# Two feed-forward layers: another order for the first token tile, the token forms and the first products of the down projection

## The chip, the cores and the metric

The kernel runs on one core of one Trainium2 chip. The time is that of the device in microseconds (us), the median of several executions, lower being better. All sums and differences are held in 32-bit floats.

## The reference, cut to what matters

The whole reference is a hybrid block (feed-forward, sparse and forgetting attention, memory attention, feed-forward) and then an attention and a pooling layer, on 512 tokens of width 1024. The change concerns the two feed-forward layers (FFN1 at the start of the kernel, FFN2 in its middle), the loads ahead of FFN1, and a small table of attention biases that is made beside FFN1:

```
def rmsnorm(x, g):
    y = x32 * lax.rsqrt(jnp.mean(x32 * x32, axis=-1, keepdims=True) + RMS_EPS)
    return (y * g).astype(x.dtype)
def swiglu(h, w_gate, w_up, w_down):
    return (jax.nn.silu(h @ w_gate) * (h @ w_up)) @ w_down
x = x + 0.5 * swiglu(rmsnorm(x, ffn1_norm[l]), ffn1_w_gate[l], ffn1_w_up[l], ffn1_w_down[l])
```

D_MODEL is 1024, D_FF is 2816, so a feed-forward layer has 8 slices of 128 input features (KD) and 22 tiles of 128 hidden features (NF).

## The kernel before

Tokens lie along the free dimension, features along the 128 partitions. Every 32-bit product is made of three: each operand is split into a high and a low part of TensorE's reduced 32-bit type (`split`, L83: a copy on ScalarE (ACT) makes the high part at L78, a subtraction on VectorE (DVE) the low part at L81 or L89), and `three` (L116) issues high x high, high x low and low x high. The token tiles are `xh[k]`, `xl[k]`. A weight tile of 128 x 1024 is loaded on SyncE's queue (SP, L112), split, and used for 24 matmuls of 512 columns (`gemm_steps`, L121). There are three buffers each of raw, high and low weights (`wr`, `wh`, `wl`).

Ahead of FFN1 (L1513 on) the eight token tiles are loaded and split, the gate weights of tile 0 after token tile 0, its up weights after the last token tile. The squares of the tokens (for the norm) are made on ACT, and summed on GpSimd (POOL, L223).

`ffn` (L428) then has these stages:

- **The plain part**: hidden tiles f = 0 to 3, one gate product and one up product each, 24 matmuls of 512 columns apiece. The scale of the norm (`rstd`, L257) is taken after four slices of tile 1. `up_gate` (L438) multiplies by it, applies silu and stores the result `hx[f]`.
- **The forms** (class `Halves`, L355): sums and differences of quarters of the token matrix, called t1, t2, t3 and t4, four slices each. For each k two token tiles are loaded again from DRAM on SP's queue (L365, three buffers `g`), scaled in place on ACT, combined in four operations on DVE (L371 to L374) and split. t1 overwrites the right halves of `xh[0..3]`, `xl[0..3]`, which the plain part still reads until its end. The class is called after the plain part.
- **The seven-product part** (`seven`, L387): the other 18 hidden tiles in nine pairs, for the gate and then the up weights of a pair: seven products of 12 matmuls of 256 columns instead of eight. The order of products is raw left, t3, t2, t1, raw, t4, raw. One of its weight tiles gets its low part by a DMA on POOL's queue that accumulates (L399).
- **The down part**: first all `hx` are split (`halves`, L481: 22 splits, f = 0 on), then eight output tiles follow. The first two run side by side, eight slices of one, eight of the other, and so on. At outputs 3 and 4 FFN1 also runs `bias_rows` (L604): small loads, two small products, and a copy of the result to 128 rows in DRAM (`rep`, L619), all its DMAs on SP's queue.

TensorE (PE) runs in the order of the program; the other engines and the queues are ordered by a planner from the program's order, buffers and its own costs.

## Time and profile before

| | us |
|---|---|
| median of 3 runs | 1708.16 (1707.75 to 1710.77) |
| the profiled execution, its own time | 1711.25 |
| its span, first to last instruction | 1709.5 |
| PE busy | 1652.4 (97% of the span) |
| VectorE (DVE) busy | 1150.6 (67%) |
| ScalarE (ACT) busy | 908.5 (53%) |
| mean granted TensorE clock | 0.986 of 2.4 GHz |

PE busy time counts a matmul until its modelled end, at whatever clock it ran; so time is lost in two ways: PE idle (some 57 us in all), and PE busy at the lower clock. In the rows below times are microseconds from the span's start; a timeline row gives start, duration, engine, line, operation, output and inputs, how many, and in brackets how long the engine had been idle and what it waited for. PEld is the weight load of a matmul.

### The profile page before, as it was taken

Reading aid. Unit: us, or ns where it says so; the run is one execution under the profiler, and the core shown is the slowest. Engines: PE = TensorE matmul, PEld = TensorE weight load, DVE = VectorE, ACT = ScalarE, POOL = GpSimd, SP = SyncE. Lnnn points to the kernel's source line nnn. Section 1 sums busy time; section 2 is a strip of 40 time slices with the busy share of each in tenths; the row PEclk is TensorE's granted clock in tenths of the full one; section 3 lists DMA queues with packets and bytes.
Section 4 is the critical chain, followed back from the end, with each engine's and each line's share of the span. In section 5 each row is a group of like instructions: output and inputs, shape, how many; then the busy total and the mean of one; then the engine's idle time right before and its main releaser. Section 6 shows DMA issues by size and latency. Waiting matters only on the chain.

```text
span 1709.5 us, 25566 instructions
## 1 busy us (share of the span) xinstructions
PE 1652.4 (97%) x9596; PEld 1434.8 (84%) x9596; DVE 1150.6 (67%) x2114; ACT 908.5 (53%) x1580; POOL 308.4 (18%) x395
## 2 busy tenths in 40 slices
PE   8899999989999999999999998999999999999997
PEld 6699998778777888887988877999888888878887
DVE  7688875336786677776655457788743698866674
ACT  6566663225675566645534455666533477744343
POOL 2011100003322232203001201112011044420001
PEclk9899999999999999999999998999999999999999
DMA  7578853533343122136531545888344311143232
GB/s 233 146 180 189 188 129 107 184 101 98 109 127 125 56 75 80 32 114 207 175 133 44 204 131 145 184 182 180 93 132 128 125 62 62 63 147 116 93 118 77
DMA packets 78987, 216.92 MB, mean 127 GB/s; under 512 B 9398, under 2 KB 15368, under 8 KB 78864
## 3 DMA queue, kind: packets, MB, share of 16 engines
q1 hardware_dynamic: 61648, 175.44, 32.3%
q0 software_dynamic: 10368, 28.32, 10.0%
q10 hardware_dynamic: 6848, 11.54, 1.8%
q8 instruction: 75, 1.23, 0.3%
q14 instruction: 48, 0.39, 0.1%
HBM read 202.64 MB, written 15.24 MB: 127 GB/s over the span
## 4 chain that ended last, share of the span: by engine, by line
PE 84%; DVE 7%; ACT 3%; issue 2%; DMA 2%; POOL 1%; SPq 0%; DVEq 0%; ACTq 0%; POOLq 0%
PE mm L117 15%; PE mm L118 15%; PE mm L119 15%; PE mm L352 6%; PE sc L352 6%; PE tr L352 5%; PE pv L352 4%; DVE wl L81 1%; PE tr L119 1%; PE tr L565 1%; PE tr L117 1%; PE tr L118 1%; PE pv L321 1%; PE pv L322 1%; PE pv L323 1%
## 5 line engine op out<-in xcount | busy, mean ns | idle before, releaser
L78 ACT ACTIVATE wh<-wr 128x1024 fp32r<-128x1024 f32 (+2 forms) x256 | 256.1, 1002 | 361.5 <-PE mm L118 193.6
L81 DVE TENSOR_TENSOR wl<-wr,wh 128x1024 fp32r<-128x1024 f32 (+2 forms) x219 | 254.3, 1163 | 138.8 <-ACT wh L78 136.9
L117 PE MATMUL mm<-xh,wh 128*128 128x512 f32 x584 | 244.9, 419 | 7.1 <-ACT wh L78 5.7
L118 PE MATMUL mm<-xl,wh 128*128 128x512 f32 x584 | 233.7, 400 | 0.2
L119 PE MATMUL mm<-xh,wl 128*128 128x512 f32 x584 | 233.0, 399 | 0.0
L223 POOL TENSOR_TENSOR acc<-acc,t 128x512 f32<-128x512 f32 (+1 forms) x55 | 75.0, 1371 | 519.5 <-ACT t L222 519.3
L118 PE MATMUL mm<-h,wh 128*128 128x512 f32 x352 | 140.4, 399 | 3.6 <-DVE h L81 3.6
L117 PE MATMUL mm<-h,wh 128*128 128x512 f32 x352 | 140.2, 398 | 3.8 <-ACT wh L78 3.8
L119 PE MATMUL mm<-h,wl 128*128 128x512 f32 x352 | 140.5, 399 | 0.8 <-DVE wl L81 0.8
L117 PEld LDWEIGHTS mm<-xh,wh 128*128 128x128 f32 x584 | 112.2, 192 | 25.7 <-ACT wh L78 5.7
L119 PEld LDWEIGHTS mm<-xh,wl 128*128 128x128 f32 x584 | 111.0, 190 | 26.5 <-DVE wl L81 0.2
L118 PEld LDWEIGHTS mm<-xl,wh 128*128 128x128 f32 x584 | 111.6, 191 | 19.3 <-DVE xl L89 2.4
L78 ACT ACTIVATE ph<-tr 128x512 fp32r<-128x512 f32 (+3 forms) x136 | 63.1, 467 | 51.8 <-PE tr L565 45.3
L81 DVE TENSOR_TENSOR pl<-tr,ph 128x512 fp32r<-128x512 f32 (+3 forms) x136 | 72.0, 530 | 24.0 <-ACT ph L78 23.0
L117 PEld LDWEIGHTS mm<-h,wh 128*128 128x128 f32 x352 | 67.3, 191 | 20.1 <-ACT wh L78 4.8
L118 PEld LDWEIGHTS mm<-h,wh 128*128 128x128 f32 x352 | 67.2, 191 | 19.7 <-DVE h L81 4.3
L555 POOL TENSOR_SCALAR P<-P,sm 128x128 f32<-128x128 f32 (+1 forms) x96 | 53.6, 571 | 155.3 <-DVE sm L552 70.1
L119 PEld LDWEIGHTS mm<-h,wl 128*128 128x128 f32 x352 | 67.4, 191 | 16.5 <-DVE wl L81 1.2
L81 DVE TENSOR_TENSOR pl<-wr,ph 128x1024 fp32r<-128x1024 f32 x36 | 44.1, 1225 | 38.5 <-ACT ph L78 38.3
L546 ACT ACTIVATE P<-S,nmx 128x128 f32<-128x128 f32 (+1 forms) x96 | 53.5, 557 | 23.7 <-DVE nmx L542 21.9
L117 PE MATMUL mm<-yh,wh 128*128 128x512 f32 (+1 forms) x176 | 64.5, 366 | 0.5 <-DVE xs L1467 0.4
L118 PE MATMUL mm<-yl,wh 128*128 128x512 f32 (+1 forms) x176 | 64.4, 366 | 0.4 <-DVE yl L89 0.2
(446 smaller groups left out, 4691.6 us busy)
## 6 DMA issues: line engine op xcount, KB each, us to landing
wr<-in_mfm_dram SPq DMA_DIRECT2D x32, 512.0 KB, 3.5
wr<-in_f2gu_dram SPq DMA_DIRECT2D x26, 512.0 KB, 3.5
wr<-in_f1gu_dram SPq DMA_DIRECT2D x24, 512.0 KB, 4.2
xd<-xs ACTq DMA_DIRECT2D x40, 256.0 KB, 2.0
r<-in_f1gu_dram SPq DMA_DIRECT2D x18, 512.0 KB, 4.3
wl<-in_f1gu_dram POOLq DMA_DIRECT2D x18, 512.0 KB, 6.9
r<-in_f2gu_dram SPq DMA_DIRECT2D x18, 512.0 KB, 4.3
wl<-in_f2gu_dram POOLq DMA_DIRECT2D x18, 512.0 KB, 7.2
```

The lines of the kernel that those rows point to most:

```text
L78: nc.scalar.activation(o, i, AF.Copy, scale=scale)
L81: (eng or nc.vector).tensor_sub(o, i, h.bitcast(F32))
L117: nc.tensor.matmul(o, sh, mh, start=start, stop=False)
L118: nc.tensor.matmul(o, sh, ml, start=False, stop=False)
L119: nc.tensor.matmul(o, sl, mh, start=False, stop=stop)
L223: (nc.vector if last else nc.gpsimd).tensor_add(acc, acc, q[:, :n])
L321: mm(b, sh[k][:, tk], hi[:, c], start=first, stop=False, skip_group_check=True)
L322: mm(b, sh[k][:, tk], lo[:, c], start=False, stop=False, skip_group_check=True)
L323: mm(b, sl[k][:, tk], hi[:, c], start=False, stop=last, skip_group_check=True)
L352: nc.tensor.matmul(o, w[:, c], x, start=start and k + z == 0, stop=stop and k == 3 and z == 2, skip_group_check=True)
L546: nc.scalar.activation(w, sc[:, :n], AF.Exp, scale=-1.0, bias=nmx[:, i : i + 1], accum_out=sm[:, i : i + 1])
L555: nc.gpsimd.tensor_scalar(w, w, sm[:, z : z + 1], 1.0, op0=OP.mult, op1=OP.mult)
```

## The change

- **First tile**: nine matmuls on zeros stand first. The token tiles and both weight tiles of f = 0 are loaded and split in a fixed order: token 0; the first quarters of gate and up weights; token 1; the second quarters; tokens 2 and 3; the halves left; tokens 4 to 7. Gate and up products go slice by slice in turns. The gains are loaded on ACT's queue. The squares come after the copy of tile 1's last weights and are summed on DVE; the loads of `ident` and the causal mask come after them. The norm's scale is taken in tile 2 of FFN1 (tile 1 of FFN2, as before).
- **Forms**: `Halves` is called after tile 1 of the plain part instead of after tile 3, in both layers. Its loads use the buffers `xs`. t1 is kept as a 32-bit tile, and split into `xh`, `xl` (`finish`) after the plain part.
- **Plain tiles' results** are split at once (`first`), so `halves` has 18 tiles left, f = 4 on.
- **Down part**: the two first outputs alternate after 4, 4, 8 and 6 slices instead of 8, 8 and 6.
- `bias_rows` runs at tiles 2 and 3 of the plain part instead of at outputs 3 and 4 of the down part.

```diff
+WARM = 9
...
-            split(hi[:, c], lo[:, c], raw[:, c])
+            last_high[0] = copy(hi[:, c], raw[:, c])
+            low(lo[:, c], raw[:, c], hi[:, c])
...
+            self.first = [up.tile([P, 256], F32, name=nm("t1")) for _ in range(4)]
             for k in range(4):
                 ab = []
                 for m in (k, k + 4):
-                    x = up.tile([P, S], F32, tag="g", bufs=3, name=nm("g"))
+                    x = tp.tile([P, S], F32, tag="xs", bufs=3, name=nm("xs"))
                     nc.sync.dma_start(x, cur[0][P * m : P * (m + 1), :])
                     copy(x, x, gcol(gain, m))
                     ab.append(x)
                 a, b = ab
                 one, two = slice(0, 256), slice(256, 512)
-                u, v = tmp(), tmp()
-                nc.vector.tensor_sub(u[:, one], a[:, one], a[:, two])
-                nc.vector.tensor_add(u[:, two], b[:, two], u[:, one])
+                u, v = self.first[k], tmp()
+                t = tmp()
+                nc.vector.tensor_sub(u, a[:, one], a[:, two])
                 nc.vector.tensor_sub(v[:, one], a[:, two], b[:, two])
-                nc.vector.tensor_sub(v[:, two], b[:, one], u[:, two])
-                split(xh[k][:, two], xl[k][:, two], u[:, one])
-                split(*self.t["t2"][k], u[:, two])
+                nc.vector.tensor_add(t[:, one], b[:, two], u)
+                nc.vector.tensor_sub(v[:, two], b[:, one], t[:, one])
                 split(*self.t["t3"][k], v[:, one])
+                split(*self.t["t2"][k], t[:, one])
                 split(*self.t["t4"][k], v[:, two])
+
+        def finish(self):
+            for k in range(4):
+                split(xh[k][:, 256:], xl[k][:, 256:], self.first[k])
...
+        half = (lead + NF) // 2
+        hold = 2 if ws else 1
+        extra = aside() if aside else iter(())
...
+            first = [[lp.tile([P, S], F32R, name=nm("h")) for _ in range(2)]
+                     for _ in range(1, lead)]
+            r = new_rstd()
+            first.insert(0, [tp.tile([P, S], F32R, tag="rstd", bufs=3, name=nm("h"))
+                             for _ in range(2)])
...
-                nc.vector.tensor_mul(hx[f], a, pu)
...
-                x = Halves(up, gain)
...
+                h = tmp()
+                nc.vector.tensor_mul(h, a, pu)
+                split(*first[f], h)
+                hh.append(first[f][0])
+                hl.append(first[f][1])
+
+            forms = ExitStack()
+            held = []
+            for f in range(lead):
+                if f in (2, 3):
+                    next(extra, None)
+                pg, pu = (pvb(), pvb()) if f == hold == 2 else (mmb(), trb())
+                if ws and f == 0:
+                    both = [gemm_steps(b, None, KD, xh, xl, ws=w) for b, w in zip((pg, pu), ws)]
+                    for _ in range(KD):
+                        for steps in both:
+                            advance(steps, 1)
+                    for steps in both:
+                        drain(steps)
+                    held.append((f, pg, pu))
+                    continue
+                steps = gemm_steps(pg, wgu[f, 0], KD, xh, xl)
+                if f == hold:
+                    advance(steps, 4)
+                    rstd(acc, r)
+                    for h in held:
+                        up_gate(*h)
+                drain(steps)
+                gemm(pu, wgu[f, 1], KD, xh, xl)
+                if f < hold:
+                    held.append((f, pg, pu))
+                else:
+                    up_gate(f, pg, pu)
+                if f == 1:
+                    if ws:
+                        acc = acc(last_high[0])
+                    rp = forms.enter_context(area("raw", "right"))
+                    up = forms.enter_context(area("up", "right"))
+                    x = Halves(up, gain)
+            x.finish()
...
+                g1, g2 = (tp.tile([P, S], F32, tag="xs", bufs=3, name=nm("g")) for _ in range(2))
...
-                halves(p1, range(half))
+                halves(p1, range(lead, half))
...
-                        for n in (KD, KD, NF - 2 * KD):
+                        for n in (4, 4, KD, NF - 2 * KD):
...
-                        if m in (3, 4):
-                            next(extra, None)
...
-        hot = [tmp()[:33, :320] for _ in range(2)]
+        hot = [new_acc()[:33, :320] for _ in range(2)]
...
-    nc.sync.dma_start(gains[:, : len(GAINS) * KD], A["gains"])
+    nc.scalar.dma_start(gains[:, : len(GAINS) * KD], A["gains"])
...
+    begun = ExitStack()
+    xp0 = begun.enter_context(area("x0", "right"))
+    with area("w0") as wp0:
+        warm = wp0.tile([P, S], BF16, name="warm")
+        nc.vector.memset(warm, 0.0)
+        wb = pvb()
+        for _ in range(WARM):
+            nc.tensor.matmul(wb, warm[:, :P], warm, start=True, stop=True)
         x0 = [xp0.tile([P, S], F32, name=f"x0{k}") for k in range(KD)]
 
+        raw = [wp0.tile([P, DM], F32, name=f"w0{i}") for i in range(2)]
+        ws = [(wp.tile([P, DM], F32R, tag="wh", name=nm("wh")),
+               wp.tile([P, DM], F32R, tag="wl", name=nm("wl"))) for _ in range(2)]
+
+        keep = tc.keep_in_program_order
+
+        def begin(hi, lo, raw, src, gain=1.0):
+            keep(nc.sync.dma_start(raw, src))
+            last = keep(copy(hi, raw, gain))
+            keep(nc.vector.scalar_tensor_tensor(lo, raw, gain, hi.bitcast(F32), op0=OP.mult,
+                                                op1=OP.subtract))
+            return last
+
         def token_tile(k):
-            nc.sync.dma_start(x0[k], A["xT"][P * k : P * (k + 1), :])
-            split(xh[k], xl[k], x0[k], gcol("ffn1", k))
-
+            return begin(xh[k], xl[k], x0[k], A["xT"][P * k : P * (k + 1), :], gcol("ffn1", k))
+
+        cuts = [slice(0, 256), slice(256, 512), slice(512, 1024)]
         token_tile(0)
-        ws.append(weights(A["f1gu"][0, 0], cuts=2))
-        for k in range(1, KD):
-            token_tile(k)
-        ws.append(weights(A["f1gu"][0, 1], cuts=2))
-        acc0 = new_acc()
-        for k in range(KD):
-            square_in(acc0, x0[k], k == 0)
+        for z, c in enumerate(cuts):
+            for i in range(2):
+                begin(ws[i][0][:, c], ws[i][1][:, c], raw[i][:, c], A["f1gu"][0, i][:, c])
+            for k in ((1,), (2, 3), (4, 5, 6, 7))[z]:
+                token_tile(k)
...
-    nc.sync.dma_start(ident, A["c_ident"])
-    nc.vector.tensor_copy(ident_bf, ident)
     rep = dr.tile([8, P, 640], F32, name="rep")
-    cm = tmp()
-    nc.sync.dma_start(cm[:, :P], A["c_causal"])
-    nc.vector.tensor_copy(cmask_bf, cm[:, :P])
-
-    acc = ffn(A["f1gu"], A["f1d"], acc0,
+
+    def first_acc(behind):
+        acc = new_acc()
+        with tc.issue_after(behind.ins):
+            for k in range(KD):
+                square_in(acc, x0[k], k == 0, True)
+        parts = pieces(acc)
+        begun.close()
+        nc.sync.dma_start(ident, A["c_ident"])
+        nc.vector.tensor_copy(ident_bf, ident)
+        cm = tmp()
+        nc.sync.dma_start(cm[:, :P], A["c_causal"])
+        nc.vector.tensor_copy(cmask_bf, cm[:, :P])
+        return parts
+
+    acc = ffn(A["f1gu"], A["f1d"], first_acc,
               lambda m, t, a: prep_tile(m, t, gcol("mix", m), a), "ffn1", ws=ws, aside=bias_rows)
     with ExitStack() as late:
         tokens = mem_tokens(late)
```

## Rows read from the trace of the kernel before

**Rows 1.** The page, part 1: busy time, share of the span, instructions.
```profile
PE 1652.4 (97%) x9596; PEld 1434.8 (84%) x9596; DVE 1150.6 (67%) x2114; ACT 908.5 (53%) x1580; POOL 308.4 (18%) x395
```
**Rows 2.** Waits of PE over the span: in total, times, longest.
```profile
PE mm L352 <- ACT t L78: 15.0, 4, 4.2
...
PE mm L118 <- DVE h L81: 3.6, 2, 1.8
```
**Rows 3.** Timeline of the first 25 us: PE, DVE and POOL.
```profile
4.67 0.75 DVE L89 SCALAR_TENSOR_TENSOR xl<-x,gains,xh 128x512 fp32r<-128x512 f32 x1 [1.93 <-ACT xh L78]
...
5.73 0.79 PE L117 MATMUL mm<-xh,wh 128*128 128x512 f32 x1 [5.73 <-ACT wh L78]
...
9.89 7.80 DVE L89 SCALAR_TENSOR_TENSOR xl<-x,gains,xh 128x512 fp32r<-128x512 f32 x6 [0.38 <-ACT xh L78]
...
13.61 0.63 PE L119 MATMUL mm<-xh,wl 128*128 128x512 f32 x1
...
14.04 0.63 PE L117 MATMUL mm<-xh,wh 128*128 128x512 f32 x1
...
15.67 6.56 POOL L223 TENSOR_TENSOR acc<-acc,t 128x512 f32<-128x512 f32 x4 [0.89 <-ACT t L222]
...
17.39 0.40 PE L119 MATMUL mm<-xh,wl 128*128 128x512 f32 x1
```
**Rows 4.** Timeline of PE: where tile 1 of FFN1 begins.
```profile
24.70 0.40 PE L117 MATMUL mm<-xh,wh 128*128 128x512 f32 x1
```
**Rows 5.** Transfer rate of the first 60 us, in 40 slices of 1.5 us.
```profile
GB/s 0 112 335 270 290 399 407 397 394 246 19 0 0 0 44 327 307 403 324 284 232 344 385 251 262 276 223 64 109 288 280 202 0 0 76 186 251 266 234 74
```
**Rows 6.** Timeline of PE around the first seven products of FFN1.
```profile
58.90 0.28 PE L352 MATMUL mm<-xh,wh 128*128 128x256 f32 x1
...
81.00 0.28 PE L352 MATMUL sc<-xh,wh 128*128 128x256 f32 x1
...
90.95 0.28 PE L352 MATMUL mm<-xh,wh 128*128 128x256 f32 x1
```
**Rows 7.** Timeline of PE: the first seven products of FFN2 begin and end.
```profile
1022.43 0.28 PE L352 MATMUL mm<-xh,wh 128*128 128x256 f32 x1
...
1045.72 0.28 PE L352 MATMUL sc<-xh,wh 128*128 128x256 f32 x1
```
**Rows 8.** Timeline from 54 us: the forms on DVE, their loads, the second pair's weights on ACT.
```profile
54.08 0.41 DVE L371 TENSOR_TENSOR t<-g 128x256 f32<-128x256 f32 x1
...
56.09 1.09 DVE L81 TENSOR_TENSOR t<-t,t 128x256 fp32r<-128x256 f32 x3
...
60.39 5.36 SPq L365 DMA_DIRECT2D g<-in_xT_dram  x3
...
61.99 1.04 ACT L78 ACTIVATE wl<-wr 128x1024 fp32r<-128x1024 f32 x1
```
**Rows 9.** Timeline around the start of FFN1's down part: PE and DVE.
```profile
250.10 0.40 PE L117 MATMUL mm<-h,wh 128*128 128x512 f32 x1
251.57 6.70 DVE L81 TENSOR_TENSOR h<-hx,h 128x512 fp32r<-128x512 f32 x11
252.31 0.50 PE L118 MATMUL mm<-h,wh 128*128 128x512 f32 x1 [1.82 <-DVE h L81]
...
256.29 0.40 PE L119 MATMUL mm<-h,wl 128*128 128x512 f32 x1
```
**Rows 10.** Windows: PE, PEld, DVE, ACT, POOL busy (instructions), clock, DMA share, GB/s.
```profile
1000.00:1020.00 20.00, 20.00 (x87) 16.09 (x86) 11.13 (x19) 8.74 (x13) 0.87 (x1) 1.00 0.40 106
20.00:60.00 40.00, 40.00 (x177) 32.36 (x176) 27.53 (x41) 22.73 (x32) 4.90 (x5) 1.00 0.72 213
100.00:150.00 50.00, 50.00 (x424) 50.00 (x424) 41.10 (x68) 32.94 (x43) 8.65 (x10) 1.00 0.81 186
```
**Rows 11.** DMA issues: line, KB each, us from issue to landing.
```profile
wl<-in_f1gu_dram POOLq DMA_DIRECT2D x18, 512.0 KB, 6.9
...
rep<-rb SPq DMA_DIRECT2D x1, 2560.0 KB
```

More of the change, by code (lines that the diff above doesn't have):

```diff
@@ L135, in gemm, with drain @@
         for _ in gemm_steps(*args, **kw):
+            pass
+    def drain(steps):
+        for _ in steps:
             pass
@@ L429, in ffn, with halves @@
         lead = 4
+        half = (lead + NF) // 2
         left, right = slice(0, 256), slice(256, 512)
-        half = NF // 2
-        with area("late") as lp:
+        hold = 2 if ws else 1
+        extra = aside() if aside else iter(())
+        hx, hh, hl = {}, [], []
+        def halves(pl, fs):
+            for f in fs:
+                h, l = (pl.tile([P, S], F32R, name=nm("h")) for _ in range(2))
+                split(h, l, hx[f])
+                hh.append(h)
+                hl.append(l)
+        with area("late") as lp:
+            first = [[lp.tile([P, S], F32R, name=nm("h")) for _ in range(2)]
[3 more added lines that the diff above has]
+                             for _ in range(2)])
             ahead = ExitStack()
+            for f in range(half, NF):
+                hx[f] = lp.tile([P, S], F32, name=nm("hx"))
             ap = ahead.enter_context(area("ahead"))
-            hx = [(ap if f < half else lp).tile([P, S], F32, name=nm("hx")) for f in range(NF)]
-            r = new_rstd()
+            for f in range(lead, half):
+                hx[f] = ap.tile([P, S], F32, name=nm("hx"))
             def up_gate(f, pg, pu):
@@ L481, in halves @@
-            def halves(pl, fs):
-                for f in fs:
-                    h, l = (pl.tile([P, S], F32R, name=nm("h")) for _ in range(2))
-                    split(h, l, hx[f])
-                    hh.append(h)
-                    hl.append(l)
-            hh, hl = [], []
+                h = tmp()
[4 more added lines that the diff above has]
+            forms = ExitStack()
@@ new lines, in ffn @@
+            x.finish()
+            for f in range(lead, NF, 2):
+                ba, bb = mmb(), trb()
+                ut = seven(up, rp, wgu[:, 0], f, x, ba, bb)
+                g1, g2 = (tp.tile([P, S], F32, tag="xs", bufs=3, name=nm("g")) for _ in range(2))
+                nc.vector.tensor_mul(g1[:, left], ba[:, left], r[:, left])
+                four(ba, bb, ut, g1, g2)
+                nc.vector.tensor_mul(g1[:, right], g1[:, right], r[:, right])
+                nc.vector.tensor_mul(g2, g2, r)
+                nc.scalar.activation(g1, g1, AF.Silu)
+                nc.scalar.activation(g2, g2, AF.Silu)
+                ba, bb = scb(), pvb()
+                ut = seven(up, rp, wgu[:, 1], f, x, ba, bb)
+                h1, h2 = hx[f], hx[f + 1]
+                nc.vector.tensor_mul(h1[:, left], ba[:, left], g1[:, left])
+                four(ba, bb, ut, h1, h2)
+                nc.vector.tensor_mul(h1[:, right], h1[:, right], g1[:, right])
+                nc.vector.tensor_mul(h2, h2, g2)
@@ L489, in ffn @@
+            forms.close()
             with area("one", "right") as p1:
-                halves(p1, range(half))
+                halves(p1, range(lead, half))
                 ahead.close()
@@ L505, in body @@
                         for st in steps:
-                            for _ in st:
-                                pass
+                            drain(st)
                     if m < 2:
-                        pd = first[m]
+                        pd = two[m]
                     else:
-                        if m in (3, 4):
-                            next(extra, None)
                         pd = mmb()
```

48 lines of the change are left out of this document (5 added, 43 removed).

## The prediction, made before the changed kernel was run

> **What bounds the kernel now.** I read the page first: PE is busy for 97% of the span [rows 1], so nothing but PE's idle time and its lower clock can be won without taking matmuls away, and this change takes none away. The waits of PE come next, because they say which idle time has one owner: 15.0 us in the seven-product part for ACT's forms, and twice 1.8 us in the down part for the first `h` [rows 2]. Then I went to the timeline at those places and at the start, since a wait also costs the clock that falls behind it. Four places stand out.
>
> *Start.* The first matmul comes at 5.73 us and the next ones are spread out; from about 13.6 they run without a gap of note, 0.43 us apart, and only by 17.39 has the duration fallen from 0.63 to 0.40 us [rows 3], the change from 1.2 to 2.4 GHz. Tile 1 begins at 24.70 [rows 4]. DVE is the reason for the spread: a low part takes 0.75 us alone, but six took 7.80 us, 1.30 each, in the time when POOL was adding squares [rows 3]. The transfers are not: they ran near 400 GB/s until 13.5 us and then paused for 6 us [rows 5].
>
> *First pair of FFN1.* The seven products of the first gate pair last from 58.90 to 81.00, 22.10 us; the next seven, which nothing holds up, from 81.00 to 90.95, 9.95 us [rows 6]. The loss is 12.15 us, idle and slow clock together; the longest single wait there and in FFN2 is 4.2 us [rows 2].
>
> *First pair of FFN2.* 1022.43 to 1045.72 is 23.29 us [rows 7]; minus 9.95, the loss is 13.34 us.
>
> The forms are late because they come last in the program: DVE takes up the first one at 54.08, and then the loads for the later slices wait for one of three buffers, three of them being issued between 60.39 and 65.75 [rows 8].
>
> *Start of the down part.* PE issues one matmul at 250.10, waits 1.82 us for the low part of the first `h` and is at the high clock again at 256.29 [rows 9]. Eleven matmuls lie between; from 24.70 [rows 4] to 58.90 [rows 6] there are 146 (three tiles of 48 and two for the norm), 0.234 us each, so eleven should take 2.57 us and took 6.19: a loss of 3.62 us. The same wait occurs in FFN2 [rows 2], together 7.2 us.
>
> **The change part by part.** *First tile.* 48 matmuls of 0.234 us are 11.2 us. The first one needs token 0 and a quarter of the weights, so it starts a little before today's 5.73; I say 5.3. The floor is then 16.5 us for its end, a gain of 8.2 on 24.70. The ceiling is all 48 at the low clock: at the pitch of 0.43 us [rows 3] they take 20.5 us, an end at 25.8 and a loss of 1.1. What decides between them is whether PE is fed. DVE has eight token parts of 0.75 us and, for each of two weight tiles, two quarters of 0.41 us (the price of 256 columns in [rows 8]) and a half of 0.75: 9.1 us from about 4.7, done by 14, with POOL's adds gone from beside it. That is ahead of PE, which thus soon has work without gaps and rises as it did within 3.8 us from 13.61 on [rows 3]; the nine matmuls on zeros, some 3.9 us at that pitch, run while the first loads are on the way. I take 17.5, a gain of **7.2 us**. The weights of tile 1 can land by 14 at the rate of [rows 5], so no wait follows. The squares move behind them; their sum is needed four slices into tile 2, about 14 us after the first tile's end, and eight squares and adds of about 0.6 us each fit.
>
> *Forms in FFN1.* If they are ready, the 12.15 us go. But the work moves into the plain part, where DVE was busy for 27.5 of 40 us and ACT for 22.7 [rows 10]. Added there: the forms' rest (for each k four operations of 0.41 us and four low parts of 0.36 us [rows 8], 3.1 us, of which some 4.5 of 12.4 us already fall in that window), so 8; eight adds and four `h` splits of about 0.61 us (6.70 / 11, [rows 9]), 7.3 us. That makes 42.8 us of DVE for a stretch of about 39 us; as neighbouring operations overlap by a tenth (0.69 long, 0.61 apart), it is close to full. Seven products also follow without the pause in which the second pair's weights were made: today the second pair's copy ends at 63.03 [rows 8], and its accumulating transfer takes 6.9 us [rows 11], so about 9.4 us after the first pair's start at best, against the 9.95 us that the first seven last. What is late next is therefore DVE's last forms or that transfer. The remainder lies between 0 and 12.15; with DVE full but not beyond, I take 4.5 and count **7.65 us** gained.
>
> The copy to `rep` now falls into that stretch: 2.5 MB [rows 11], 6.5 us of transfer at 400 GB/s [rows 5], at a time when 0.72 of the DMA engines are busy [rows 10]; no row shows it beside the accumulating loads. It costs between 0 and 6.5 us, and I have put 1 us of the 4.5 on it, as SP's loads run ahead. SP's queue behind `rep`'s wait for its small stores holds the raw weights of the following pairs; they are loaded a pair ahead. The Trainium skill ("DMA: Bandwidth & Descriptors", Queues, rings and completion order) says that a DMA engine takes its queues in turn, packet by packet, so the accumulating loads would keep every second turn beside `rep`. By that rule the stall would be nearer to zero than to the upper bound, and the sum would be lower by that 1 us.
>
> The bias products on PE are moved, not added: zero. The splits of four `h` and of t1 are moved too; t1's wait for the last reading of `xh[0..3]`, which ends half a product before the plain part does, and its product is the fourth.
>
> *Forms in FFN2.* DVE is busy for 11.1 of 20 us [rows 10] in the plain part; the forms and splits add 14.8 us to some 36 us, about 0.9 in all, without squares and without `rep`. Bounds 0 and 13.34; remainder 1.5, so **11.8 us** gained.
>
> *Down part.* The four first `h` are there, and 24 matmuls (two outputs, four slices) are 5.6 us of work that waits for nothing. The `halves` begin as before and need 1.82 us and then 0.61 us apiece, while PE takes 1.4 us for each. Bounds 0 and 7.2; both losses go: **7.2 us**. If the planner puts the splits later, 3.8 us of cover remain.
>
> Sum: 7.2 + 7.65 + 11.8 + 7.2 = 33.9 us. The profiled execution took 1711.25 us, so its like would take 1677.4; it lies 3.1 us above the median, and from the median of 1708.16 I come to **1674 us**. About 0.2%, 3.4 us, is what a measurement of this kernel can tell from no change.
>
> **The rivals.** *Forms still late.* For: DVE near full in FFN1, and the loads' turn through three buffers, which the change keeps. Against: they are called two tiles, 22 us, earlier. Half of both losses staying is 12.7 instead of 6.0 us: 1681. That the change doesn't do what it says, all of both staying because the planner leaves the forms where they are, gives 1674 + 19.5 = 1693.5.
>
> *The first tile stays at the low clock.* For: today the scattered matmuls up to 13 us did. Against: DVE is ahead. The end is at 24.7 or later, the gain of 7.2 is gone: 1681. The Trainium skill ("TensorE: Matmul & The Clock Gate", A second HAM failure mode) says that short idle gaps between groups of matmuls can throw the clock back again and again; by it the slice-by-slice order would be at risk, and the scattered matmuls of [rows 3] agree.
>
> *Slower.* The token loads of the forms now stand ahead of the weights of tiles 2 and 3 in SP's queue, and each waits for a buffer that DVE frees. If the weights are late at every slice group, the plain tiles run in pieces at the low clock: 0.43 instead of 0.234 us for 144 matmuls of tiles 1 to 3 is 27.8 us in each layer, 55.6 in both, and 1674 + 55.6 = 1730. It decides from 17 us a layer, some 87 slow matmuls. Against it: today three of these loads already stand among weight loads in FFN1, and PE ran all of 20 to 60 us without a gap [rows 10].
>
> **How the numbers follow.** Forecast 0.68; forms half late 0.13; forms wholly late 0.06; low clock at the start 0.07; slower 0.04; gains and losses that cancel 0.02. So faster 0.94, same 0.02, slower 0.04. The lowest end is with no remainders and the floor of the first tile: 8.2 + 12.15 + 13.34 + 7.2 = 40.9 us, 1667, and I go to 1666. The upper end takes in the half-late forms together with the low clock, 1688; beyond it lie the wholly late forms, the slower case and the cancelling one, 0.12.
>
> **What would show it.** Right: tile 1 begins at 17 to 18 us, with DVE's low parts at 0.75 us each; the first seven products last 10 to 15 us in FFN1 and 10 to 12 in FFN2; no wait of PE for `h`. Wrong: waits of PE for ACT or DVE in the first or second pair above 5 us, matmuls of 0.63 us in the plain part, or waits for `wh` in tiles 1 to 3.

## The result, and the profile after

The changed kernel takes 1687.41 us in the median of four executions (1686.54 to 1688.53), the kernel before on the same chip 1708.85; the ratio is 0.9874, with a 95% interval of 0.9857 to 0.9891. Faster, then, by 21.4 us, where 34 were forecast. The profiled execution took 1686.54 us, its span is 1684.8, and 24.7 us lie between it and the span of before.

The page, part 1, answers to [rows 1]:
```profile
PE 1642.7 (98%) x9605; PEld 1428.6 (85%) x9605; DVE 1147.9 (68%) x2124; ACT 910.1 (54%) x1582; POOL 299.3 (18%) x388
```
The waits of PE (in total, times, longest) answer to [rows 2]:
```profile
PE mm L121 <- DVE t L471: 4.6, 1, 4.6
PE sc L653 <- DVE t L269: 4.6, 1, 4.6
...
PE tr L360 <- DVE pl L82: 2.9, 1, 2.9
PE mm L360 <- ACT wh L79: 2.1, 1, 2.1
...
PE sc L360 <- DMA wl<-in_f1gu_dram: 1.0, 1, 1.0
```
ACT's 15.0 us for the forms and DVE's 3.6 us for `h` are gone. Two new waits stand at the top, both in the plain part, one for the norm's first step (L269) and one for a gate's first step (L471).

The timeline of PE at the start answers to [rows 3, 4]:
```profile
1.34 4.02 PE L1554 MATMUL pv<-warm 128*128 128x512 bf16 x9 [1.34 <-DVE warm L1551]
4.89 0.89 PE L121 MATMUL mm<-xh,wh 128*128 128x512 f32 x1
...
6.28 0.39 PE L121 MATMUL tr<-xh,wh 128*128 128x512 f32 x1
...
18.40 0.40 PE L121 MATMUL mm<-xh,wh 128*128 128x512 f32 x1
```
The high clock is there from 6.28 instead of 17.39, and tile 1 begins at 18.40 instead of 24.70.

Stage by stage, from the starts of the stages on PE's timeline in both traces (us):

| stage | before | after | difference |
|---|---|---|---|
| start of tile 1, FFN1 | 24.70 | 18.40 | -6.30 |
| tile 1 to the first seven | 34.20 | 47.59 | +13.39 |
| first seven, FFN1 | 22.10 | 9.97 | -12.13 |
| second to fourth seven | 29.84 | 37.57 | +7.73 |
| down part, FFN1 | 141.99 | 130.33 | -11.66 |
| from there to the first seven of FFN2 | 630.34 | 627.46 | -2.88 |
| first seven, FFN2 | 23.29 | 14.47 | -8.82 |
| down part, FFN2 | 133.92 | 130.33 | -3.59 |

The front of FFN1 (the first four lines) gave nothing, +2.7 us in all; what was won there came back in the next stages. How it came back is seen on PE's timeline at 46 to 53 us:
```profile
46.71 1.23 PE L653 MATMUL sc<-acc,tbl 33*8 33x320 f32 x2 [4.57 <-DVE t L269]
52.53 0.77 PE L121 MATMUL mm<-xh,wh 128*128 128x512 f32 x1 [4.59 <-DVE t L471]
53.10 0.63 PE L122 MATMUL mm<-xl,wh 128*128 128x512 f32 x1
```
and on DVE's:
```profile
45.29 0.43 DVE L382 TENSOR_TENSOR t<-xs,xs 128x256 f32<-128x256 f32 x1 [1.26 <-ACT xs L79]
...
45.97 0.68 DVE L269 TENSOR_SCALAR t<-sc 128x512 f32<-128x512 f32 x1
...
51.69 0.69 DVE L471 TENSOR_TENSOR t<-mm,rstd 128x512 f32<-128x512 f32 x1
```
PE had summed the norm by 32.9. Its first DVE step runs 13 us later, right behind the forms of slice k=3 (L382), which themselves waited for tokens. Until the gates behind the norm are through, the banks for the bias products and for tile 3 are not free. A slow stretch follows, matmuls of 0.63 us at 1.2 GHz from 53.10 to about 57 us; the windows (PE, PEld, DVE, ACT, POOL busy, clock as a share of 2.4 GHz, DMA share, GB/s) show the granted clock:
```profile
40.00:50.00 10.00, 3.37 (x11) 1.08 (x9) 6.47 (x15) 5.99 (x9) 0.86 (x1) 0.68 0.65 158
50.00:60.00 10.00, 7.47 (x23) 5.98 (x24) 7.74 (x13) 5.01 (x7) 0.00 (x0) 0.64 0.16 52
```
The third seven took 16.40 us. The timeline there, of SP's queue, ACT and PE:
```profile
59.50 0.68 SPq L656 DMA_DIRECT2D rb<-t  x2
61.27 0.76 SPq L657 DMA_DIRECT2D rep<-rb  x1
64.05 10.49 SPq L405 DMA_DIRECT2D r<-in_f1gu_dram  x2
...
83.22 0.63 ACT L79 ACTIVATE h<-r 128x512 fp32r<-128x512 f32 x1 [2.40 <-DMA r<-in_f1gu_dram]
...
90.77 0.50 PE L360 MATMUL mm<-t,wh 128*128 128x256 f32 x2 [2.05 <-ACT wh L79]
```
and of the DMA issues from 58 to 68 us, the first of these loads (KB, us from issue to landing):
```profile
r<-in_f1gu_dram SPq DMA_DIRECT2D x1, 512.0 KB, 19.2
```
The next raw weights (`r`) stand behind the broadcast to `rep` in SP's queue. They are issued 2.8 us after it and land only 19.2 us later, where the median of these loads over the whole execution is 4.5; ACT waits for them, and PE for ACT. The second seven, before it, lost 1.2 us, with a wait of 1.0 us for an accumulating load: beside the broadcast these took 9.1 us to land (two of them, 64 to 78 us), by the page 6.9.

The down part of FFN1 won 8.1 us more than FFN2's; 1.17 of it are the bias products that left. The rest is a wait which the prediction had passed over, in the trace of before (SP, ACT and PE of its timeline around output 5):
```profile
321.26 0.77 SPq L619 DMA_DIRECT2D rep<-rb  x1
323.94 9.60 SPq L112 DMA_DIRECT2D wr<-in_f1d_dram  x3
...
348.28 0.72 ACT L78 ACTIVATE xh<-xs,gains 128x512 fp32r<-128x512 f32 x1 [13.21 <-DVE xs L517]
...
349.43 2.72 ACT L78 ACTIVATE wh<-wr 128x1024 fp32r<-128x1024 f32 x3
...
350.52 0.50 PE L117 MATMUL mm<-h,wh 128*128 128x512 f32 x1 [3.80 <-ACT wh L78]
```
The next weights (`wr`) are again behind the broadcast, and two of them land 13.0 us after their issue in the median, at 339.0 and 340.5. That is still before PE ends output 5, at 346.7. PE waits because ACT, in order, has the copy of output 5's own result (`xh`), which needs PE and then DVE, ahead of the copies of these weights (`wh`).

### The profile page after: what moved, and what is told of

Same layout as the page of the kernel before. It is cut to its first block, busy times and chain, and to the rows that moved or that the text cites. A ratio compares the mean times of both kernels' runs of the same rounds, so it can differ in the third digit from the quotient of the medians.

```text
span 1684.8 us, 25596 instructions
## 1 busy us (share of the span) xinstructions
PE 1642.7 (98%) x9605; PEld 1428.6 (85%) x9605; DVE 1147.9 (68%) x2124; ACT 910.1 (54%) x1582; POOL 299.3 (18%) x388
## 3 DMA queue, kind: packets, MB, share of 16 engines
q8 instruction: 75, 1.23, 0.3%
## 4 chain that ended last, share of the span: by engine, by line
PE 83%; DVE 6%; ACT 4%; issue 3%; POOL 2%; DMA 1%; SPq 0%; DVEq 0%; ACTq 0%; POOLq 0%
PE mm L121 15%; PE mm L122 15%; PE mm L123 15%; PE sc L360 6%; PE mm L360 6%; PE pv L360 4%; PE tr L360 4%; PE tr L603 1%; PE pv L329 1%; PE tr L121 1%; PE tr L122 1%; PE tr L123 1%; PE pv L330 1%; PE pv L331 1%; DVE wl L82 1%
## 5 line engine op out<-in xcount | busy, mean ns | idle before, releaser
L82 DVE TENSOR_TENSOR wl<-wr,wh 128x1024 fp32r<-128x1024 f32 (+2 forms) x215 | 249.4, 1161 | 140.8 <-ACT wh L79 139.3
L121 PE MATMUL mm<-xh,wh 128*128 128x512 f32 x576 | 240.9, 418 | 4.7 <-DVE t L471 4.6
L122 PE MATMUL mm<-xl,wh 128*128 128x512 f32 x576 | 229.3, 398 | 0.4 <-DVE xl L1566 0.3
L123 PE MATMUL mm<-xh,wl 128*128 128x512 f32 x576 | 228.6, 397 | 0.0
L231 POOL TENSOR_TENSOR acc<-acc,t 128x512 f32<-128x512 f32 (+1 forms) x48 | 65.0, 1362 | 492.4 <-ACT t L230 492.4
L122 PE MATMUL mm<-h,wh 128*128 128x512 f32 x352 | 138.5, 393 | 0.0
L121 PE MATMUL mm<-h,wh 128*128 128x512 f32 x352 | 138.3, 393 | 0.0
L122 PEld LDWEIGHTS mm<-xl,wh 128*128 128x128 f32 x576 | 109.7, 190 | 18.5 <-DVE xl L1566 1.8
```

Source lines behind the costliest of these rows:

```text
L82: (eng or nc.vector).tensor_sub(o, i, h.bitcast(F32))
L121: nc.tensor.matmul(o, sh, mh, start=start, stop=False)
L122: nc.tensor.matmul(o, sh, ml, start=False, stop=False)
L123: nc.tensor.matmul(o, sl, mh, start=False, stop=stop)
L231: (nc.vector if last else nc.gpsimd).tensor_add(acc, acc, q[:, :n])
```

## The experiments

Twelve kernels, each with one profile. The last three of the table have four or five executions each, the others one, so that their time alone says little on a few us. Times stand beside the kernel before on the same chip, which differed by up to 3 us. Three runs that leave FFN1's front as it is in the changed kernel are not in the table; their times stand with them. The stages are in us, from PE's timeline (sevens 2 to 4 are 29.85 where nothing holds them up):

| kernel | plain part | first seven | sum | sevens 2 to 4 | down starts | down, FFN1 | time (before) |
|---|---|---|---|---|---|---|---|
| before | 34.20 | 22.10 | 56.30 | 29.84 | 250.10 | 141.99 | |
| changed | 47.59 | 9.97 | 57.56 | 37.57 | 252.78 | 130.33 | 1687.41 (1708.85) |
| norm's own buffer | 42.52 | 9.97 | 52.49 | 39.23 | 249.09 | 130.33 | 1685.29 (1709.57) |
| slices 2, 3 later | 36.75 | 13.66 | 50.41 | 38.14 | 246.00 | 130.33 | 1684.67 (1709.57) |
| slice 3 later | 41.03 | 9.94 | 50.97 | 38.67 | 247.33 | 130.33 | 1684.63 (1706.95) |
| all forms later | 35.55 | 22.41 | 57.96 | 38.37 | 254.04 | 130.33 | 1688.20 (1709.57) |
| bias in down, SP | 48.60 | 9.94 | 58.54 | 29.90 | 245.68 | 138.91 | 1689.41 (1709.57) |
| bias in down, POOL | 47.29 | 9.97 | 57.26 | 29.90 | 244.87 | 132.55 | 1682.19 (1706.95) |
| combined A | 35.84 | 13.74 | 49.58 | 29.90 | 237.06 | 132.55 | 1678.03 (1706.76) |
| combined B | 35.55 | 13.86 | 49.41 | 29.90 | 236.70 | 132.55 | 1679.93 (1706.76) |
| A, with low parts on POOL | 39.42 | 16.23 | 55.65 | 29.85 | 243.25 | 132.54 | 1677.76 (1708.75) |

**A buffer of its own for the norm.**
```diff
-                    rstd(acc, r)
+                    b = total(acc)
+                    v = lp.tile([P, S], F32, name=nm("n"))
+                    nc.vector.tensor_scalar(v, b, 1.0 / DM, EPS, op0=OP.mult, op1=OP.add)
...
```


> Edit: the norm's first DVE step (mean square plus eps) gets a buffer of its own instead of one of the five shared temporaries; the forms of all four slices stay where they are in the program and DVE's work is the same. Theory 1 (DVE takes its work in order, and the norm stands there behind the forms of slice k=3, whose tokens land late, because it needs a shared temporary): the norm is done in front of that slice, both waits of 4.6 us at tile 3 (for the norm's first step and for its last one) go, the stretch from tile 1 to the first seven products shrinks from 47.6 to 35 to 38 us, the first seven stay at 10 to 11 us, the end comes 10 to 12 us earlier. Theory 2 (DVE simply has too much to do in the plain part): what the plain part wins comes back as a wait of the first seven for the forms; the end comes less than 3 us earlier. Theory 3 (the bias products at tile 3 make the wait): no change.

Half of it came true: the wait for the norm's first step is gone, the one for the gate stays. DVE and PE of this run's timeline:
```profile
45.68 0.42 DVE L382 TENSOR_TENSOR t<-xs,xs 128x256 f32<-128x256 f32 x1 [1.35 <-ACT xs L79]
...
46.36 0.68 DVE L471 TENSOR_TENSOR t<-mm,rstd 128x512 f32<-128x512 f32 x1
...
47.19 0.76 PE L121 MATMUL mm<-xh,wh 128*128 128x512 f32 x1 [4.81 <-DVE t L471]
```
The norm now ends ahead of slice 3, and the next instruction that needs a shared temporary, the gate, stands behind it instead. The first seven stayed at 9.97 us, so the 5.1 us came back nowhere in front of them: DVE being full (theory 2) was not the cause of this wait. The end came only 1.3 us earlier, not 10 to 12: 1.7 us went in the second to fourth seven and 1.5 between the layers.

**Two slices of the forms later.**
```diff
-            for k in range(4):
+            self.gain = gain
+            self.make((0, 1))
+        def make(self, ks):
+            for k in ks:
...
+                if f == hold:
+                    x.make((2, 3))
```


> Edit: the forms of slices 0 and 1 stay behind tile 1, those of slices 2 and 3 are made behind the gated tile that the norm opens. Theory 1 (order on DVE): no wait of PE above 1 us at tile 3, plain part of FFN1 35 to 38 us, first seven 10 to 13 us, end 9 to 12 us earlier. Theory 2 (DVE full): the forms of slices 2 and 3 come too late, the first seven last 15 us or more and the end comes less than 4 us earlier. Theory 3 (bias products): the waits stay at 4.6 us each. In FFN2, where the forms' place moves as well (they come behind the same tile 1, after its gate), no difference above 1 us by any theory.

DVE and PE of this run's timeline:
```profile
34.72 0.68 DVE L269 TENSOR_SCALAR t<-sc 128x512 f32<-128x512 f32 x1
...
43.64 0.47 PE L121 MATMUL mm<-xh,wh 128*128 128x512 f32 x1 [1.16 <-DVE t L475]
```
The norm's step runs at 34.72 instead of 45.97 and tile 3 waits 1.2 us: theory 1. The bias products are still there and cost their 1.2 us, so theory 3 falls. The first seven give 3.7 us back. The down part starts 6.8 us earlier, but the end came only 1.9 us earlier, against the expected 9 to 12: 3.1 us went between the layers, where the edit changes nothing, and in FFN2 the first seven took 15.98 us instead of 14.47, against the expectation; the wait there is nearly the same (3.0 us for `pl` instead of 2.9). Both are slow clock, see the last section.

**One slice later.** As above with `(0, 1, 2)` and `(3,)`.

> Edit: as the run that split the forms in halves, but only slice 3's forms are made behind the gated tile that the norm opens; slices 0, 1 and 2 stay behind tile 1. There the plain part fell to 36.8 us and the first seven took 13.7 us, since slices 2 and 3 came late. Theory 1 (order on DVE, the late slice being k=3 alone): plain part 36 to 38 us and first seven 10 to 11.5 us, so the first seven end 2 to 3 us earlier than there. Rival (the last tokens' load stands in SP's queue behind a weight load that waits for its buffer, wherever the forms stand): the first seven still take 13 us or more.

The first seven are whole, but tile 3 waits 2.9 us for the gate: ACT has the late tokens of slice 3 ahead of the gate's Silu. The sum is that of two slices, 51.0 against 50.4 us.

**All forms one tile later.**
```diff
                         acc = acc(last_high[0])
+                if f == hold:
                     rp = forms.enter_context(area("raw", "right"))
                     up = forms.enter_context(area("up", "right"))
```


> Edit: all forms of FFN1 are made one tile later, behind the gated tile that the norm opens; FFN2 is unchanged. Theory 1 (order on DVE): no wait above 1 us at tile 3, plain part 35 to 38 us; DVE then has some 22 us for the 12.4 us of forms and 7 us of gates and splits, so the first seven products last 10 to 14 us; the end comes 7 to 12 us earlier. Theory 2 (DVE full): the 11 us come back in front of the first seven (19 us or more) and the end stays within 3 us. Theory 3 (bias products): waits as before, plain part 46 us or more.

The waits at tile 3 are gone, as theory 1 has it, and all of it returns one stage on, as theory 2 has it. This run's timeline of PE in the first seven:
```profile
59.14 0.58 PE L360 MATMUL mm<-t,wh 128*128 128x256 f32 x1 [2.74 <-ACT t L79]
...
66.02 1.18 PE L360 MATMUL mm<-t,wh 128*128 128x256 f32 x2 [5.20 <-ACT t L79]
```
In these runs forms that come too early block the gates and forms that come too late block the sevens; in two pieces they cost least.

**The bias work back in the down part.**
```diff
-                if f in (2, 3):
-                    next(extra, None)
...
+                        if m in (3, 4):
+                            next(extra, None)
...
-        hot = [new_acc()[:33, :320] for _ in range(2)]
+        hot = [tmp()[:33, :320] for _ in range(2)]
```


> Edit: the bias work (its products, its two small stores and the broadcast of 2.5 MB to rep) goes back to outputs 3 and 4 of the down part, on SP's queue as in the kernel before. Theory 1 (norm behind the forms on DVE): the wait of the third plain tile for the norm's last step stays, or moves to tile 3 of the plain part, and the plain part still lasts 43 us or more. Theory 3 (bias products make the wait in the plain part): the plain part falls to 35 us. Theory 4 (the broadcast and its small stores on SP's queue hold up the weights): the second and third pairs of seven products go from 11.2 and 16.4 back to 9.95 us each, and the down part of FFN1 grows from 130.3 to 137 to 139 us, with a wait of PE for wh near output 5; against theory 4, the pairs stay at 11 and 16 us.

Theory 4's numbers came: the second to fourth seven are back at 9.97 us each, and in this run's list of PE's waits the 3.8 us of before are back, in the down part:
```profile
PE mm L121 <- DVE t L471: 11.4, 1, 11.4
PE mm L121 <- ACT wh L79: 3.8, 1, 3.8
```
The plain part still waits, 11.4 us in one piece, which is the second sign against theory 3.

**The same, its transfers on POOL's queue.**
```diff
-            nc.sync.dma_start(rb[:, 320 * z : 320 * z + 320], sb[0:8, :320])
-        nc.sync.dma_start(rep, rb.unsqueeze(1).to_broadcast([8, P, 640]))
+            nc.gpsimd.dma_start(rb[:, 320 * z : 320 * z + 320], sb[0:8, :320])
+        nc.gpsimd.dma_start(rep, rb.unsqueeze(1).to_broadcast([8, P, 640]))
```


> Edit: the bias work goes back to outputs 3 and 4 of the down part as in the run before this one, but its two small stores and the broadcast of 2.5 MB are issued on POOL's queue instead of SP's. In the run on SP's queue the down part of FFN1 grew from 130.3 to 138.9 us, with a wait of PE of 3.8 us for ACT's high part of a weight. Theory 4a (what costs is SP: the stores' wait for DVE and the broadcast's wait for the stores hold up the weight loads queued behind them): no such wait, down part 131 to 132 us, sevens of the first two pairs 9.95 us each. Theory 4b (what costs is the transfer itself, which takes the DMA engines' time from the weights): the wait stays at 3 to 4 us and the down part at 137 to 139 us.

No wait for `wh`; the down part takes 132.55 us, of which 1.17 are the products. So the bias work costs 6.4 us more on SP's queue than on POOL's (138.91 - 132.55), for the same 2.5 MB. This run's DMA issues give the broadcast's time to landing, and its timeline the order on ACT:
```profile
rep<-rb POOLq DMA_DIRECT2D x1, 2560.0 KB, 20.0
...
327.97 1.06 ACT L79 ACTIVATE wh<-wr 128x1024 fp32r<-128x1024 f32 x1 [1.81 <-issue]
...
340.16 0.72 ACT L79 ACTIVATE xh<-xs,gains 128x512 fp32r<-128x512 f32 x1 [1.63 <-DVE xs L555]
```
The transfer takes 20.0 us here and PE does not wait, so theory 4b falls. Theory 4a names the right queue, but not the right step. SP issues the next weights at 315.89 with the bias work on its queue and at 315.07 without it; what differs is the landing, 14.7 against 7.0 us after the issue (median of two each). Even so they landed, the first at 332.6, before PE ended output 5 at 338.7. The 3.8 us come of the order on ACT: `xh` ahead of the next weights with the bias work on SP's queue, as in the kernel before, and the weights first here. That the planner chose the order by the queue is argued, not shown, and the late landing without ACT's order was not tried. In the changed kernel's third seven it is the landing itself that ACT waits for. Whether POOL's queue would also do in the plain part, where it carries the accumulating loads, was not tried.

**FFN2's forms one tile earlier.**
```diff
-                if f == 1:
+                if f == (1 if ws else 0):
```


> Edit: in FFN2 alone the forms are made behind tile 0 instead of tile 1 (FFN1 unchanged). Theory A (the forms of FFN2 end too late by the 4.5 us that the first seven lost, since the tokens' loads start too late): the first seven fall from 14.5 to 10 to 11 us, the plain part stays at 39.8 us, the end comes about 4 us earlier. Theory B (the loads wait for buffers and weights in SP's queue whatever the place in the program): the first seven stay at 14 us, and weights of tiles 1 and 2 come late, plain part 42 us or more.

The time is 1692.95 us (1706.95 before, one execution). The first seven fell to 9.97 us, and the end came 6.4 us later than in the changed kernel's trace, which neither theory had. This run's timeline of ACT and PE at FFN2's norm:
```profile
985.02 0.72 ACT L79 ACTIVATE xs<-xs,gains 128x512 f32<-128x512 f32 x1 [1.80 <-DMA xs<-xd]
985.65 0.61 ACT L79 ACTIVATE t<-acc 128x512 fp32r<-128x512 f32 x1
...
986.32 0.79 PE L261 MATMUL sc<-t,ones_r 128*128 128x512 f32 x1 [6.66 <-ACT t L79]
```
It is FFN1's mechanism on another engine: ACT splits the sum of squares behind the last tokens of the forms.

**One warm-up matmul.** `WARM = 1` for 9.

> Edit: one warm-up matmul on zeros instead of nine. If the nine matmuls are what brings the high clock into the first tile, the first 5 us of real matmuls run 0.63 us long instead of 0.39 and tile 1 begins 1.5 to 4 us later than 18.4 us. If the feeding of PE is the bound (parts by DVE and ACT), tile 1 begins within 0.5 us of 18.4.

The first matmuls run at the low clock, as this run's timeline of PE shows:
```profile
6.50 0.63 PE L121 MATMUL tr<-xh,wh 128*128 128x512 f32 x1
...
9.91 0.63 PE L123 MATMUL tr<-xh,wl 128*128 128x512 f32 x1
```
yet tile 1 begins at 18.82, 0.42 us later than in the changed kernel; the time is 1687.76 us (1706.95 before, one execution). Feeding is the bound there. What the nine matmuls are worth is small and not exact: the other kernels that keep them begin tile 1 at 17.7 to 18.5.

**Outputs by 8, 8 and 6 slices.** `(KD, KD, NF - 2 * KD)` for `(4, 4, KD, NF - 2 * KD)`.

> Edit: the two alternating outputs of the down part advance by 8, 8 and 6 slices as in the kernel before, instead of 4, 4, 8 and 6; the four first h are still split in the plain part. If the alternation by fours is needed as cover: the first output asks for the fifth h some 2.8 us after the start instead of 5.6 us, its split then is not done, a wait of 0.5 to 2 us comes back in each layer with the slow clock behind it, and the down parts take 132 to 134 us instead of 130.3. If the early splits alone suffice (1.8 us for the fifth h, 0.6 us apiece after it, against 0.7 us of PE per slice of one output): no wait, 130.3 us in both layers.

No wait, 130.33 us in both down parts; the time is 1687.60 us (1708.75 before, one execution). The early splits alone removed the wait for `h`; the alternation by fours does nothing here.

**Combined A and B.** A: slices 2 and 3 later in FFN1 alone, bias work in the down part on POOL's queue. B: the bias work as in A, and slices 2 and 3 of FFN1's forms, and all forms of FFN2, directly behind the gates that the norm releases. B's edit, against the changed kernel:
```diff
                     for h in held:
                         up_gate(*h)
+                    if ws:
+                        x.make((2, 3))
+                    else:
...
+                        x = Halves(up, gain)
```


> Edit: two parts of earlier runs together: in FFN1 the forms of slices 2 and 3 are made behind the gated tile that the norm opens (FFN2 unchanged), and the bias work stands in the down part with its stores and broadcast on POOL's queue. If the causes found are separate ones (order on DVE and ACT in the plain part, stores and broadcast on SP's queue), the gains add: plain part 35 to 37 us, first seven 13 to 14 us (slices 2 and 3 late), all later sevens 9.95 us, down part of FFN1 131 to 133 us, down part begins at 237 to 239 us instead of 252.8, time 1671 to 1677 us. Rival (the late forms of the first seven then stand against something else, or the broadcast was needed early): less than 9 us gained, 1678 us or more.

> Edit: as the kernel before it in this call, but the forms of slices 2 and 3 of FFN1 are made directly behind the gates that the norm releases (in the middle of tile 2, not behind its gate), and in FFN2 all forms are made at the same place, behind the gate of tile 0 in the middle of tile 1. If the loads' place in the program sets when forms are ready: first seven of FFN1 10 to 12 us, first seven of FFN2 10 to 11.5 us instead of 14.5, with the norm in FFN2 not delayed; time 4 to 7 us under the kernel before it, 1664 to 1671 us. Rival (in order, DVE and ACT then come late to the gate of tile 2 or tile 1, and the banks are late): a wait of PE at tile 3 of 3 us or more in one layer, time the same or higher than the kernel before it.

A has a ratio of 0.9834 to the kernel before (0.9821 to 0.9848), below the whole interval of the changed kernel. FFN1 came out as the sum of the parts; the time is at the rival's bound, since 3.9 us went again behind the down part (mostly slow clock of the kind in the last section). B has 0.9844 (0.9831 to 0.9858), no better: FFN2's first seven take 9.97 us, but tile 3 there waits 4.0 us for a gate, 6.7 with the slow clock behind it. In FFN1 the first seven stayed at 13.9 us though the forms came earlier; in A the longest of their waits is for a weight's low part that DVE makes (timeline of PE):
```profile
60.66 0.38 PE L360 MATMUL tr<-t,pl 128*128 128x256 f32 x1 [1.66 <-DVE pl L82]
```

**A, with low parts on POOL.**
```diff
-                split(*first[f], h)
+                copy(first[f][0], h)
+                low(first[f][1], h, first[f][0], nc.gpsimd if f >= 2 else None)
...
+                low(xl[k][:, 256:], self.first[k], xh[k][:, 256:], nc.gpsimd)
```


> Edit: as the first of the two combined kernels (forms of slices 2 and 3 behind the gate, bias work in the down part on POOL's queue), and in both layers the low parts of the h of tiles 2 and 3 and of the four t1 are made by POOL instead of DVE, 2.6 us less for DVE in front of the first pair. What is left there is a wait of the first seven for a weight's low part pl, 13.7 us in FFN1 and 14.5 to 15.8 us in FFN2 instead of 9.95. If DVE's amount of work is the cause: first seven 10 to 12 us in both, time 1671 to 1675 us. Rival (DVE's operations get longer beside POOL's, as 1.30 for 0.75 us at the start of the kernel before, or POOL's own are late): first seven as they were, time within 2 us of 1678 or above.

The ratio is 0.9812 (0.9799 to 0.9825), which can't be told from A. FFN2's first seven fell to 12.55 us; in FFN1 they rose to 16.23. This run's timeline of POOL and DVE at that place:
```profile
56.84 1.55 POOL L82 TENSOR_TENSOR h<-t,h 128x512 fp32r<-128x512 f32 x1 [1.35 <-ACT h L79]
...
57.16 1.51 DVE L388 TENSOR_TENSOR t<-xs,t 128x256 f32<-128x256 f32 x1
...
58.36 2.67 POOL L82 TENSOR_TENSOR xl<-t,xh 128x256 fp32r<-128x256 f32 x3
...
58.60 2.71 DVE L82 TENSOR_TENSOR t<-t,t 128x256 fp32r<-128x256 f32 x3
```
An operation of 0.42 us takes DVE 1.51 beside POOL's, and three of 1.09 ([rows 8]) take 2.71, so at this place what DVE is spared it loses again. The Trainium skill ("GPSIMD Engine Reference", Specifications) says that POOL shares its SBUF interfaces with DVE and contends with DVE instructions that have two SBUF inputs; these rows agree. Of the 6.1 us that FFN1's front lost against A, 2.5 are in the first seven. The other 3.6 are in the plain part, ahead of POOL's first low part: there the norm's last step stood on DVE behind a form whose tokens came late, once more the order.

## Why the prediction was right, and where it was not

The sign and the range held, and the gain was 21.4 of 34 us. That the range held is in part luck. The time, 1687.41, lies 0.6 us inside its upper end, which stood for half-late forms together with a low clock at the start, and that is not what happened. FFN1's front, in the sum with 7.65 us, lost 9.0 instead, and gains that no term had (8.0 in FFN1's down part, 2.9 between the layers) made up for much of it. Of the signs named for being right, tile 1 (18.40, not 17 to 18) and FFN2's first seven (14.47, not 10 to 12) missed. By its own terms:

*First tile, 7.2.* It gave 6.3. The steps were right: high clock early, DVE and ACT ahead, POOL out of the way. The start was 4.89 for 5.3, and from there to tile 1 it took 1.3 us more than the term allowed, some of it the first matmuls at the low clock and the rest small gaps of feeding. The rival of the low clock did not come about: with gaps of up to 0.3 us in the first slices the matmuls stayed at 0.39 to 0.50 us. So what the prediction cited from the Trainium skill on oscillation ("TensorE: Matmul & The Clock Gate", A second HAM failure mode) is not seen here, and [rows 3], where the clock had not yet risen, could not bear it out.

*Forms in FFN1, 7.65.* This failed. The prediction said that what comes late next is "DVE's last forms or that transfer", and priced the remainder at the first pair. The first pair had none at all: its 12.13 us went entirely. "That transfer" was late only in the second seven, by 1.0 us and beside the broadcast; the 9.4 us put down for it come from no row, [rows 8] and [rows 11] give 11.0 after the pair's start for the kernel before. What came late was the work that the forms were now in front of, the norm and the gates, which the prediction had counted as load on DVE but not as a queue. That cost 12.2 us of plain part (13.39 less 1.17 for the bias products), two waits of 4.6 us and a slow stretch. One of the signs named for being wrong did show, matmuls of 0.63 us in the plain part; another, a wait above 5 us, looked at the wrong place. The order was at fault and not DVE's load: with the same operations, placed in two pieces, plain part and first seven together take 49.6 us (A), of which 44.2 (34.2 and 9.95) are without loss. That remainder of 5.4 us, without the bias work, is near the 4.5 of the forecast. Whether that remainder is DVE's amount of work or its order is not settled: POOL's help collided with DVE.

*`rep`, 1 us, with 6.5 as the bound.* It cost 7.7, above the bound, and the step that failed is the transfer's price: at 400 GB/s the 2.5 MB would take 6.5 us, and on POOL's queue, in another run, they took 20.0 us to land. What stood behind them in SP's queue, the raw weights, landed after 19.2 us instead of 4.5. They were hardly issued late: 64.05, against 63.33 in the run with the bias work in the down part. The prediction named these weights as queued behind the broadcast and trusted that they were loaded a pair ahead. The rule on turns among queues that it cites from the Trainium skill ("DMA: Bandwidth & Descriptors", Queues, rings and completion order), by which the time would have been 1 us lower, is about different queues; the accumulating loads did keep their turns, at 9.1 instead of 6.9 us, but the weights that cost the time stood in the broadcast's own queue.

*Bias products, "moved, not added: zero".* The products themselves moved for 1.17 us on either side. But with their transfers on SP's queue ACT's order had made a wait of 3.8 us in the down part, 6.9 us with what followed it (11.66 - 3.62 - 1.17), which went. Putting them back brought it back. So moving the bias work was worth -6.9 in one place and +7.7 in the other.

*Forms in FFN2, 11.8.* It gave 8.8; the remainder was 4.5 instead of 1.5. Earlier forms removed it and put as much or more on the norm or the gates (B, and FFN2's forms one tile earlier).

*Down part, 7.2.* 3.62 in FFN1 by the same reckoning and 3.59 in FFN2, as forecast, by the early splits alone.

*Slower.* No tile waited for its weights behind the token loads; SP's loads ran ahead, as the rows of before had shown.

The terms against what happened: 0.9 less at the start, 16.6 less in FFN1's front (7.65 forecast, 12.13 - 13.39 - 7.73 measured), 3.0 less in FFN2, 8.0 more in FFN1's down part, 2.9 more in the part between, which the change does not touch, and 0.4 more at the end. That is 9.2 us short of 33.9, the 24.7 of the traces.

## What to carry to other kernels

When work is moved to an earlier place in the program, ask on each in-order engine what now stands behind it and whether it waits there for its own inputs; a total of busy time shows nothing of this. Price a DMA by a measured time of such a transfer and by what is queued behind it on the same queue, not by its bytes at the best rate seen, and look up what the moved work delayed at its old place. When a wait names a load, look whether the load had landed: an in-order engine may hold it back behind something else. Where late inputs and an urgent chain share an engine, split the late part so that only the pieces whose data is there stand ahead of the chain.

## What the runs showed of the hardware

The same pause costs differently from run to run. At the norm in the mixer, PE waits 1.23 and then 0.90 or 0.91 us in all three of these timelines of PE. The kernel before:
```profile
806.17 0.58 PE L254 MATMUL sc<-t,ones_r 128*128 128x256 f32 x1 [0.91 <-DVE t L81]
806.55 0.63 PE L117 MATMUL mm<-yh,wh 128*128 128x512 f32 x1
```
The changed kernel:
```profile
795.73 0.39 PE L262 MATMUL sc<-t,ones_r 128*128 128x256 f32 x1 [0.91 <-DVE t L82]
795.95 0.39 PE L121 MATMUL mm<-yh,wh 128*128 128x512 f32 x1
```
The run with slices 2 and 3 later:
```profile
790.44 0.44 PE L262 MATMUL sc<-t,ones_r 128*128 128x256 f32 x1 [0.90 <-DVE t L82]
790.68 0.63 PE L121 MATMUL mm<-yh,wh 128*128 128x512 f32 x1
```
In the first and the third the clock falls to the low level for some six to eight matmuls, in the second it does not; the work and the waits there are the same, and what else differs than the moment these rows do not show. The Trainium skill ("TensorE: Matmul & The Clock Gate", What's actually happening) says that the activity is judged on a rhythm of the chip's own, which does not start with the program; these rows fit that. Two such places gave the changed kernel all of the 2.9 us between the layers (1.5 near 474 us and 1.4 here), and the run above lost 1.5 and 1.6 us at the same two. FFN2's first seven, with a wait of about 3 us for `pl`, lasted from 14.3 to 16.0 us over the runs that leave FFN2 as it is. One execution's time is therefore a weak verdict on an edit worth a few us here; the length of the stage that was edited is a better one.

A broadcast of 2.5 MB from DRAM to DRAM took 20.0 us to land on POOL's queue (the run with the bias work in the down part). Loads of 512 KB behind it on the same queue, SP's in three other runs, landed 13.0 to 19.2 us after their issue, loads on another queue beside it 7.0 to 9.1, against medians of 4.5 (SP) and 6.9 (POOL, accumulating) over the changed kernel's execution.
